# Group A's softmax denominators as pairs of 64-column products, GpSimd's sums of squares tied to the evacuation, and an earlier bias row

## The chip, the cores and the metric

The kernel is one program on 8 cores of one Trainium2 chip. Each core works on its own 2048 of the 16384 positions. The metric is the time of the slowest core, in microseconds on the device; lower is better. A core's own span is about 1 us shorter than the time reported. Some executions fall in a slow state: the cores of one die run at a lower granted clock and the time is 4 to 20% longer. Such executions are left out of all comparisons. In them the cores of the other die are often untouched (granted clock 0.99 or more), and the span of such an *undisturbed core* may still be read. I use the median of these spans, because the slowest of eight cores depends much on chance.

A "unit" below is one step of the attention loop: one head (in group B a pair of heads) by 512 of the core's 2048 queries. Each of the two head groups has 32 units.

## The reference, cut to what matters

```python
# group A: 8 heads of 128, dilated causal attention, mixture of three patterns (window, dilation)
A_PATTERNS = ((128, 1), (512, 4), (2048, 16))
# per pattern: o, running max, l = p.sum(-1) ...
w = l * jnp.exp(mx - mx.max(0))                            # softmax denominators on a common scale
ya = (w[..., None] * o).sum(0) / w.sum(0)[..., None]
# group B: 16 query heads of 64, causal sliding window, two key/value heads, a learned sink per head
# both groups: rms_norm (a sum of squares over all heads of the group), concatenate, project
y = jnp.concatenate([rms_norm(ya, g_mix_a), rms_norm(yb, g_mix_b)], axis=-1)
mix = jnp.einsum('bse,ed->bsd', y, w_out)
x = layer_norm(ALPHA * x + mix); x = layer_norm(ALPHA * x + swiglu(x))
```

What matters: each query needs the sum of its probabilities (the denominator) over all three patterns, the quotient, and the sum of squares of the quotients over all heads.

## The kernel before

A core first makes V and K of both groups, then runs group B's 32 units, group A's 32 units, the out projection, and the feed-forward part. The query projections of later heads (16 products of 512 columns, 3.6 us) are woven into the units to fill TensorE. When they run out, a unit is shorter.

The denominators are made on TensorE, as the probabilities (keys on the rows) times a matrix of ones. In group A the matrix is 128x128, so each denominator appears in all 128 rows, ready to be multiplied elementwise:

```python
        def mm_l():                                        # one pattern of one unit, 1024 columns of p
            ...
            for half in range(2):
                ...
                nc.tensor.matmul(l3[...main part...], k.ones, pm[:, :, :, mo:mo + m], start=st, stop=False)
                ins = nc.tensor.matmul(l3[:, :, me:me + m], k.ones, pe_, start=False, stop=...)   # the short rest
        S_.pe(mm_o, [pb[1], bv_], [k.bBK[b_o]])            # probabilities times V
        S_.pe(mm_l, [pb[1], k.bones], [k.bBK[b_l]])        # probabilities times ones

    def a_evac(h, c):                                      # the unit's end: 1/l = exp(-log l), then the quotient
        S_.act(lambda: nc.scalar.activation(out=ls, in_=lb, func=AF.Ln), [bLB], [bls])
        S_.act(lambda: nc.scalar.activation(out=ls, in_=ls, func=AF.Exp, scale=-1.0), [bls], [bls])
        S_.dve(lambda: nc.vector.tensor_tensor(out=yc, in0=ob, in1=ls, op=ALU.mult), [bOB, bls], [], [byc])
        ...
        sqq.append(lambda: a_square(h, c, yc, byc))        # run in the next unit: ScalarE squares, GpSimd adds

    for u in range(32):                                    # group A
        for p_ in range(3):
            ... next scores ...; a_PV(h, c, pats[p_], ...)
        a_evac(h, c)
        run(dveq, 4)                                       # rope of a projected query, on VectorE
        proj(u + 32 + LEAD, mid=(lambda: reduce_b(u)) if u < 4 else None)
```

`reduce_b` is an fp32 product of ones with group B's sums of squares; it uses the denominators' PSUM bank (`LB`) in the middle of the projections of A's first four units.

The softmax here doesn't subtract the row's maximum and nothing guards it: scores larger than these inputs give would overflow.

## Time and profile before

| | before |
|---|---|
| time, median of 3 runs | 2778.67 us (2778.12 to 2779.98) |
| spans of the cores in the profiled run | 2775.0 to 2779.8 us |
| start to first V product; from there to first K product; from there to first query projection | 13.4; 59.9; 401.2 us |
| query projection and group B | 195.2 us |
| group A: units 0 to 3; 4 to 25; 26 to 31 | 35.7; 166.9; 32.3 us |
| out projection; feed-forward; end | 230.1; 1614.2; 27.6 us |

The rows from the third on are medians over the eight cores of the profiled run, from first product to first product of each stage. The waits of TensorE in group A's first 26 units (view: waits of the slowest core between 660 and 870 us; columns: who waited, for whom, total us, times, longest):

```profile
PE sp L897 <- DVE arena L355: 2.4, 2, 1.2
PE sp L1089 <- DVE arena L1059: 0.5, 1, 0.5
PE sp L1089 <- DVE arena L1051: 0.3, 1, 0.3
```

These are all but a 0.2 us wait in over 200 us, and all of them lie before 677 us: at the end of group B and in A's first unit. The body of A is a closed chain of TensorE work, 7.57 us a unit; only the instructions themselves can shorten it.

### The profile page before, as it was taken

What the parts mean: (1) busy time and instruction counts of PE and PEld (TensorE: products, weight loads), DVE (VectorE), ACT (ScalarE), POOL (GpSimd) and SP (SyncE); (2) the same over time, 40 slices, a digit from 0 to 9 for tenths busy, and PEclk for the clock granted to TensorE, in tenths of its full rate; (3) what the DMA queues carried; (4) which work ended last, traced back from release to release, by engine and by line L of the source; (5) the groups of instructions that cost most, each with busy time, mean ns of one, the idle gap of its engine ahead of it and who ended that gap; (6) DMA issues with size and microseconds to landing.
All of it is one profiled execution on the core that took longest, in us unless ns stands there. A gap on an engine that the chain in (4) does not pass through costs nothing.

```text
span 2779.8 us, 41976 instructions; the slowest of 8 cores (2775.0 to 2779.8 us)
## 1 busy us (share of the span) xinstructions
PE 2722.1 (98%) x14991; PEld 1297.4 (47%) x14991; DVE 1989.9 (72%) x2758; ACT 842.8 (30%) x1229; POOL 569.0 (20%) x588
## 2 busy tenths in 40 slices
PE   8999999999999999999999999999999999999995
PEld 3444444445666444444444444444444444444442
DVE  4756665898888736788866666766988765666767
ACT  0312222787666227333200121111333100112115
POOL 3100000132111557411100011056000000000165
PEclk9999999999999999999999999999999999999998
DMA  9964135568657649799999877888899798555733
GB/s 151 188 117 91 48 86 135 114 121 150 135 133 189 204 138 254 129 157 149 150 165 188 168 112 115 134 210 223 161 172 172 136 200 190 83 88 91 163 125 121
DMA packets 254163, 407.23 MB, mean 146 GB/s; under 512 B 91971, under 2 KB 129988, under 8 KB 253382
## 3 DMA queue, kind: packets, MB, share of 16 engines
q0 software_dynamic: 92336, 193.64, 46.4%
q1 hardware_dynamic: 146070, 179.44, 22.9%
q10 hardware_dynamic: 15552, 31.46, 3.6%
q8 instruction: 122, 2.00, 0.3%
q14 instruction: 83, 0.68, 0.1%
HBM read 490.84 MB, written 104.27 MB: 214 GB/s over the span
## 4 chain that ended last, share of the span: by engine, by line
PE 86%; DMA 6%; DVE 4%; issue 2%; ACT 1%; SPq 0%; DVEq 0%; ACTq 0%; POOLq 0%
PE sp L1565 51%; PE sp L897 8%; PE sp L1371 8%; PE sp L636 6%; PE sp L572 5%; DMA z2s<-arena 3%; PE sp L518 2%; PE sp L1089 1%; DMA vs<-arena 1%; DMA x1h<-arena 1%; PE sp L1107 1%; PE sp L940 1%; PE sp L966 1%; PE sp L616 1%; DMA ka<-arena 1%
## 5 line engine op out<-in xcount | busy, mean ns | idle before, releaser
L1565 PE MATMUL sp<-arena 128*128 128x512 f16 x7408 | 1600.5, 379 | 1.6 <-DVE arena L1839 0.6
L1565 PEld LDWEIGHTS sp<-arena 128*128 128x128 f16 (+1 forms) x7408 | 724.4, 98 | 878.1 <-issue 6.1
L1839 DVE TENSOR_TENSOR arena<-sp,arena 128x512 f32<-128x512 f32 (+1 forms) x348 | 236.6, 689 | 159.9 <-PE sp L1565 143.1
L1925 DVE TENSOR_TENSOR arena<-arena,sp 128x512 f32<-128x512 f32 x257 | 169.7, 683 | 141.6 <-PE sp L1565 141.2
L897 PE MATMUL sp<-arena 128*128 128x512 bf16 x1024 | 236.8, 379 | 3.0 <-DVE arena L355 3.0
L140 POOL DMA_DIRECT2D arena<-wup x88 | 66.5, 756 | 773.0 <-DVE arena L1578 445.6
L1371 PE MATMUL sp<-arena 128*128 128x512 bf16 x1024 | 221.8, 379 | 2.2 <-DVE arena L1360 2.2
L636 PE MATMUL sp<-arena 128*128 128x512 bf16 x1024 | 222.2, 379 | 0.0
L1873 ACT ACTIVATE arena<-sp 128x512 f32<-128x512 f32 x86 | 51.3, 597 | 419.1 <-PE sp L1565 419.1
L362 ACT ACTIVATE arena<-sp,arena 64x512 f32<-64x512 f32 x136 | 92.7, 682 | 274.4 <-PE sp L636 232.4
L1414 POOL TENSOR_TENSOR arena<-arena 128x512 f32<-128x512 f32 x117 | 149.3, 1276 | 113.0 <-DVE arena L1925 74.0
L1413 ACT ACTIVATE arena<-arena 128x512 f32<-128x512 f32 x117 | 73.7, 630 | 283.3 <-DVE arena L1925 136.8
L1586 DVE TENSOR_TENSOR arena<-arena 128x2048 f16<-128x2048 bf16 (+1 forms) x118 | 159.5, 1352 | 0.0
L1371 PEld LDWEIGHTS sp<-arena 128*128 128x128 bf16 x1024 | 100.1, 98 | 124.2 <-issue 4.6
L1578 DVE TENSOR_TENSOR arena<-arena 128x2048 f16<-128x2048 bf16 (+1 forms) x118 | 157.3, 1333 | 0.0
L1839 DVE TENSOR_TENSOR arena<-arena 128x512 f16<-128x512 f32 (+1 forms) x304 | 155.1, 568 | 1.1 <-DMA x1h<-arena 0.9
L636 PEld LDWEIGHTS sp<-arena 128*128 128x128 bf16 x1024 | 99.9, 98 | 119.7
L572 PE MATMUL sp<-arena 128*128 128x512 f16 (+1 forms) x672 | 149.9, 382 | 3.9 <-DVE arena L582 3.7
L1416 POOL TENSOR_TENSOR arena<-arena 128x512 f32<-128x512 f32 x117 | 150.8, 1290 | 9.2 <-ACT arena L1413 8.5
L897 PEld LDWEIGHTS sp<-arena 128*128 128x128 bf16 x1024 | 95.5, 98 | 120.7 <-issue 12.2
L1836 ACT ACTIVATE arena<-sp 128x512 f32<-128x512 f32 x90 | 53.5, 597 | 276.0 <-PE sp L1565 248.5
L1048 ACT ACTIVATE arena<-sp 128x1024 bf16<-128x1024 f32 x96 | 97.4, 1020 | 68.3 <-PE sp L1042 56.5
(153 smaller groups left out, 2601.7 us busy)
## 6 DMA issues: line engine op xcount, KB each, us to landing
arena<-wup POOLq DMA_DIRECT2D x88, 1024.0 KB, 12.7
arena<-wdn POOLq DMA_DIRECT2D x22, 1408.0 KB, 17.3
z2s<-arena SPq DMA_DIRECT2D x39, 512.0 KB, 13.8
arena<-wob SPq DMA_DIRECT2D x32, 512.0 KB, 5.5
arena<-xres SPq DMA_DIRECT2D x32, 512.0 KB, 6.5
x1s<-arena ACTq DMA_DIRECT2D x64, 256.0 KB, 7.0
arena<-z2s SPq DMA_DIRECT2D x29, 512.0 KB, 13.7
arena<-wdb POOLq DMA_DIRECT2D x10, 1408.0 KB, 10.9
```

Source lines behind the costliest of these rows:

```text
L572: ins = nc.tensor.matmul(bank(k, bk), w[:, c, :], m[:, c, :], start=(first and c == 0), stop=(last and c == 7), skip_group_check=True)
L636: ins = nc.tensor.matmul(bank(k, bk), wk[h][:, kc, :], x[:, kc, :], start=(kc == 0), stop=(kc == KC - 1))
L897: ins = nc.tensor.matmul(bank(k, bk), w[:, kc, :], x[:, kc, :], start=(kc == 0), stop=(kc == KC - 1))
L1048: S_.act(lambda: nc.scalar.activation(out=p, in_=sp[:, :], func=AF.Exp, scale=scA), spb[s], [bp])
L1371: ins = nc.tensor.matmul(bank(k, bk), w[:, kc, :], y[:, kc, hh * 512:(hh + 1) * 512], start=(first and i == 0), stop=(last and i == len(kc ...
L1414: S_.pool(lambda: nc.gpsimd.tensor_tensor(out=za, in0=za, in1=z, op=ALU.add), [bz, bza], [bza])
L1416: ss["pend"] = [lambda: S_.pool(lambda: nc.gpsimd.tensor_tensor(out=qa, in0=qa, in1=sq, op=ALU.add), [bsq, bqa], [bqa])]
L1565: ins = nc.tensor.matmul(bank(k, bk), w, x, start=(first and i == 0), stop=(last and i == len(ws) - 1), skip_group_check=True)
L1578: S_.dve(lambda: nc.vector.tensor_tensor(out=v, in0=w[:, 0:n, :], in1=w[:, n:2 * n, :], op=ALU.add), [bw], [b])
L1586: S_.dve(lambda: nc.vector.tensor_tensor(out=v, in0=w[:, :, 0:128], in1=w[:, :, 128:256], op=ALU.subtract), [bw], [b])
L1839: S_.dve(lambda: nc.vector.tensor_tensor(out=o, in0=a, in1=b, op=op), [ba, bb], [bo])
L1925: S_.dve(lambda: nc.vector.tensor_tensor(out=v, in0=v, in1=o, op=op), [b, bo], [b])
```

## The change

The intent, in four parts.

1. In 26 of A's 32 units the ones matrix becomes 64 columns wide, and the unit's queries are split in two halves whose products run side by side in the two column halves of the array. Half as many columns are streamed.
2. The denominators then lie as 64 rows x 256 columns per half. The evacuation becomes a log of 128x256 written back to PSUM and four exponentials of 64x256.
3. GpSimd's additions of squares in both groups wait for the end of the exponential of the next evacuation, so that they no longer collide with VectorE's masks.
4. At the start, the V bias row is loaded first, in one transfer, and V's outgoing tiles get a ring of nine buffers in place of five.

```diff
@@ start
+    S_.dma("sp", k.bvrow[0][0:1, :], k.bv_d, [], [k.bvrow[1]], "bv")          # now ahead of five small loads
...
-                ct["v"] = nx("vo", 5)
+                ct["v"] = nx("vo", 9)
@@ group B's and group A's sums of squares (A's shown)
-                S_.pool(lambda: nc.gpsimd.tensor_tensor(out=ac, in0=ac, in1=sq, op=ALU.add), [SQ[1], bacc[c]], [bacc[c]])
+                poolq.append(lambda bls: S_.pool(lambda: nc.gpsimd.tensor_tensor(... same ...), [SQ[1], bacc[c], bls], [bacc[c]]))
@@ group A's denominators
+    L2 = 26
...
+            def mm(e, o_, r, stop):
+                ins = nc.tensor.matmul(o_, k.ones[:, 0:64], r, start=st[e], stop=stop, skip_group_check=True)
...
+            for half in range(2):
...
+                for e in range(2):
+                    mm(e, le[e][:, :, mo:mo + 128 - m]..., pm[:, :, ae[e], mo:mo + m], False)
+                for e in range(2):
+                    ins = mm(e, le[e][:, :, me:me + m], pe_[:, ae[e]], last and half == 1)
...
-        S_.pe(mm_l, [pb[1], k.bones], [k.bBK[b_l]])
+        S_.pe(mm_l2 if 4 * h + c < L2 else mm_l, [pb[1], k.bones], [k.bBK[b_l]])
@@ evacuation
+        if 4 * h + c < L2:
+            S_.act(lambda: nc.scalar.activation(out=lb[:, 0:256], in_=lb[:, 0:256], func=AF.Ln), [bLB], [bLB])
+            for i, (e, d) in enumerate(((0, 0), (0, 1), (1, 0), (1, 1))):
+                S_.act(lambda e=e, d=d: nc.scalar.activation(out=ls[64 * d:64 * d + 64, 256 * e:256 * e + 256],
+                             in_=lb[64 * e:64 * e + 64, 0:256], func=AF.Exp, scale=-1.0), [bLB], ...)
+        else:
...                                                                           # as before
+        while poolq:
+            poolq.pop(0)(bls)
```

More of the change, by code (lines that the diff above doesn't have):

```diff
@@ L327, in persist @@
     assert P.o <= FREE
+    o = XO + 2 * X_SLOT
+    k.bvrow = (view(k, o, VW, F32), S_.buf("bvrow", o, o + 4 * VW))
+    S_.dma("sp", k.bvrow[0][0:1, :], k.bv_d, [], [k.bvrow[1]], "bv")
+    S_.dve(lambda: nc.vector.memset(k.onesf, 1.0), [], [k.bonesf])
     for v, d in ((k.bqk, k.bqk_d), (k.bsw, k.bsw_d), (k.gmix, k.gmix_d), (k.lnp, k.lnp_d), (k.esink, k.sinks_d)):
@@ L330, in persist @@
     S_.dve(lambda: nc.vector.memset(k.ones, 1.0), [], [k.bones])
-    S_.dve(lambda: nc.vector.memset(k.onesf, 1.0), [], [k.bonesf])
-    S_.act(lambda: nc.scalar.activation(out=k.esink, in_=k.esink, func=AF.Exp), [bs], [bs])
-    S_.dve(lambda: nc.vector.tensor_scalar(out=k.gmix, in0=k.gmix, scalar1=32.0, scalar2=None, op0=ALU.mult), [bs], [bs])
 XO = 4096
@@ L422, in phase1 @@
     xq, bxq = P("xq", 8 * 256, F16)
+    o_r = P.o
     xr, bxr = P("xr", 16 * 256, F16)
@@ L471, in phase1 @@
         S_.dma("pool", wk[h], k.wk_d[h], [], [bwk[h]], "wk%d" % h)
-    S_.dma("sp", T1[0][0][0:1, :], k.bv_d[:, 0:512], [], [T1[0][1]], "bv0")
-    S_.dma("sp", T1[1][0][0:1, :], k.bv_d[:, 512:1024], [], [T1[1][1]], "bv1")
-    S_.dma("sp", T2[0][0][0:1, 0:128], k.bv_d[:, 1024:1152], [], [T2[0][1]], "bv2")
-    for i, (v, b, n) in enumerate((T1[0] + (512,), T1[1] + (512,), T2[0] + (128,))):
-        S_.pe(lambda i=i, v=v, n=n: nc.tensor.matmul(bank(k, 7 - i)[:, 0:n], k.onesf[0:1, :], v[0:1, 0:n], start=True, stop=True),
-              [b, k.bonesf], [k.bBK[7 - i]])
+    for i, n in enumerate((512, 512, 128)):
+        S_.pe(lambda i=i, n=n: nc.tensor.matmul(bank(k, 7 - i)[:, 0:n], k.onesf[0:1, :], k.bvrow[0][0:1, 512 * i:512 * i + n], start=True, stop=True),
+              [k.bvrow[1], k.bonesf], [k.bBK[7 - i]])
         S_.act(lambda i=i, n=n: nc.scalar.activation(out=bv[:, 512 * i:512 * i + n], in_=bank(k, 7 - i)[:, 0:n], func=AF.Copy),
                [k.bBK[7 - i]], [bbv] if i == 0 else [], [bbv] if i else [])
+    bs = k.bsmall
+    S_.act(lambda: nc.scalar.activation(out=k.esink, in_=k.esink, func=AF.Exp), [bs], [bs])
+    S_.dve(lambda: nc.vector.tensor_scalar(out=k.gmix, in0=k.gmix, scalar1=32.0, scalar2=None, op0=ALU.mult), [bs], [bs])
     k.bvs, k.bka, k.bkb = [], [[] for _ in range(8)], []
@@ L488, in phase1 @@
           for t, o in ((0, XO + 2 * X_SLOT), (1, o_g))]
+    VW9 = VO + [(view(k, o_r + 2048 * i, 1024), S_.buf("vx%d" % i, o_r + 2048 * i, o_r + 2048 * i + 2048)) for i in range(4)]
     def v_part(t, q, bk):
@@ L495, in v_part @@
             if g == 0:
-                ct["v"] = nx("vo", 5)
-            vo, bvo = VO[ct["v"]]
+                ct["v"] = nx("vo", 9)
+            vo, bvo = VW9[ct["v"]]
             S_.dve(lambda: nc.vector.tensor_tensor(out=vo[:, c], in0=bank(k, bk), in1=p[:, c], op=ALU.add), [k.bBK[bk], bp],
@@ L696, in phase1 @@
     S_.dma("pool", k.perm, k.perm_d, [], [k.bperm], "perm")
+    bxr = S_.buf("xr", o_r, o_r + 8192)
     G[:] = [(v, S_.buf("g%d" % i, o_g + 8192 * i, o_g + 8192 * i + 8192)) for i, (v, _) in enumerate(G)]
@@ L871, in phase2 @@
     sqq = []
+    poolq = []
     peq = []
@@ L995, in sq_acc @@
             S_.act(lambda: nc.scalar.activation(out=sq, in_=src, func=AF.Square), [bsrc], [SQ[1]])
-            S_.pool(lambda: nc.gpsimd.tensor_tensor(out=av, in0=av, in1=sq, op=ALU.add), [SQ[1]] + bacc, bacc)
+            poolq.append(lambda bls: S_.pool(lambda: nc.gpsimd.tensor_tensor(out=av, in0=av, in1=sq, op=ALU.add), [SQ[1], bls] + bacc, bacc))
     k.bys = [None] * KC
@@ L1091, in mm_o, with mm_l2 @@
             return ins
+        def mm_l2():
+            st = [first, first]
+            def mm(e, o_, r, stop):
+                ins = nc.tensor.matmul(o_, k.ones[:, 0:64], r, start=st[e], stop=stop, skip_group_check=True)
+                st[e] = False
+                return ins
+            le = [lb[64 * e:64 * e + 64, 0:256].rearrange("p (a m) -> p a m", a=2) for e in range(2)]
+            ae = [slice(2 * e, 2 * e + 2) for e in range(2)]
+            if pat == 2:
+                p4 = p.rearrange("p (a f n) -> p a f n", a=4, f=2)
+                for f in range(2):
+                    for e in range(2):
+                        ins = mm(e, le[e], p4[:, ae[e], f, :], last and f == 1)
+                return ins
+            n, w, m = (3, 128, 32) if pat == 1 else (15, 32, 8)
+            pm = p[:, 2 * w:1024].rearrange("p (j a m) -> p j a m", j=n, a=4)
+            for half in range(2):
+                pe_ = p[:, w * (1 - half):w * (1 - half) + w].rearrange("p (a m) -> p a m", a=4)
+                mo = m * half
+                me = 128 - m if half == 0 else 0
+                for e in range(2):
+                    mm(e, le[e][:, :, mo:mo + 128 - m].rearrange("p a (j m) -> p j a m", j=n), pm[:, :, ae[e], mo:mo + m], False)
+                for e in range(2):
+                    ins = mm(e, le[e][:, :, me:me + m], pe_[:, ae[e]], last and half == 1)
+            return ins
         def mm_l():
@@ L1118, in a_evac @@
         ob, lb, bOB, bLB = bank(k, b_o), bank(k, b_l), k.bBK[b_o], k.bBK[b_l]
-        S_.act(lambda: nc.scalar.activation(out=ls, in_=lb, func=AF.Ln), [bLB], [bls])
-        S_.act(lambda: nc.scalar.activation(out=ls, in_=ls, func=AF.Exp, scale=-1.0), [bls], [bls])
+        if 4 * h + c < L2:
+            S_.act(lambda: nc.scalar.activation(out=lb[:, 0:256], in_=lb[:, 0:256], func=AF.Ln), [bLB], [bLB])
+            for i, (e, d) in enumerate(((0, 0), (0, 1), (1, 0), (1, 1))):
+                S_.act(lambda e=e, d=d: nc.scalar.activation(out=ls[64 * d:64 * d + 64, 256 * e:256 * e + 256], in_=lb[64 * e:64 * e + 64, 0:256],
+                                                             func=AF.Exp, scale=-1.0), [bLB], [] if i else [bls], [bls] if i else [])
+        else:
+            S_.act(lambda: nc.scalar.activation(out=ls, in_=lb, func=AF.Ln), [bLB], [bls])
+            S_.act(lambda: nc.scalar.activation(out=ls, in_=ls, func=AF.Exp, scale=-1.0), [bls], [bls])
+        while poolq:
+            poolq.pop(0)(bls)
         if h < 7:
@@ L1145, in a_square @@
             else:
-                S_.pool(lambda: nc.gpsimd.tensor_tensor(out=ac, in0=ac, in1=sq, op=ALU.add), [SQ[1], bacc[c]], [bacc[c]])
+                poolq.append(lambda bls: S_.pool(lambda: nc.gpsimd.tensor_tensor(out=ac, in0=ac, in1=sq, op=ALU.add), [SQ[1], bacc[c], bls], [bacc[c]]))
     def reduce_a(t):
```

## The prediction

> **What bounds the kernel now.** I read the page's busy line first, then the stretches (busy time by window), then the waits of TensorE by stage, then the timeline of one unit per stage, because the change touches four stages: the start, group B's attention, group A's attention, and the few units that end it.
>
> The busy line, and two stretches of A (columns: stretch, length, then PE, PEld, DVE, ACT, POOL busy):
>
> ```profile
> PE 2722.1 (98%) x14991; PEld 1297.4 (47%) x14991; DVE 1989.9 (72%) x2758; ACT 842.8 (30%) x1229; POOL 569.0 (20%) x588
> ...
> 740.00:800.00 60.00, 60.00 (x682) 40.08 (x679) 50.95 (x71) 36.20 (x48) 11.16 (x10) 1.00 0.65 147
> ...
> 870.00:917.00 47.00, 39.23 (x463) 26.12 (x462) 41.34 (x60) 31.52 (x45) 9.54 (x7) 1.00 0.89 249
> ```
>
> TensorE is the bound, with 58 us idle in the span. In the body of A it never idles: a unit takes 7.57 us and only fewer or shorter TensorE instructions shorten it. In A's last 47 us, where no projections are left, it idles 7.8 us behind VectorE (88% busy). There VectorE's work counts.
>
> One unit of A, the last pattern's denominators (L1107, L1110), then the evacuation:
>
> ```profile
> 740.32 0.37 PE L1107 MATMUL sp<-arena 128*128 128x480 bf16 x1
> 740.52 0.18 PE L1110 MATMUL sp<-arena 128*128 128x32 bf16 x1
> 740.55 0.36 PE L1107 MATMUL sp<-arena 128*128 128x480 bf16 x1
> 740.75 0.18 PE L1110 MATMUL sp<-arena 128*128 128x32 bf16 x1
> 740.78 3.61 PE L897 MATMUL sp<-arena 128*128 128x512 bf16 x16
> 741.04 1.23 DVE L1051 TENSOR_TENSOR arena<-arena 128x1024 bf16<-128x1024 bf16 x1
> 741.29 0.60 ACT L1119 ACTIVATE arena<-sp 128x512 f32<-128x512 f32 x1
> 741.98 0.63 ACT L1120 ACTIVATE arena<-arena 128x512 f32<-128x512 f32 x1
> ```
>
> Start to start, this pattern's ones products hold TensorE 740.78 - 740.32 = 0.46 us; the same reading gives 0.43 (two 512-column products, L1098) and 0.44 us for the other two patterns: 1.33 us a unit.
>
> Group B already makes its ones products as 64-column pairs, so it prices the new form:
>
> ```profile
> 594.21 0.61 PE L940 MATMUL sp<-arena 64*128 64x128 bf16 x10
> 594.75 0.63 PE L966 MATMUL sp<-arena 128*64 128x128 bf16 x10
> 595.21 0.60 PE L982 MATMUL sp<-arena 128*64 128x384 bf16 x8
> 595.75 1.90 PE L897 MATMUL sp<-arena 128*128 128x512 bf16 x8
> ```
>
> Each of the first three blocks streams 1024 columns in each half of the array. A 512-column product takes 0.2155 us, so 1024 take 0.43. The blocks take 0.54, 0.46 and 0.54 us. The middle one, followed by the same shape of array (128*64), costs 0.03 over; the two after which the shape changes cost 0.11 over. In the individual starts every pair lies 3 ns apart, so the halves do run side by side, and each of the three changes of shape in a unit (128*128 to 64*128, to 128*64, to 128*128) costs 0.093 to 0.098 us.
>
> **What the Trainium skill says.** "TensorEngine Tiling (Array Packing)", Key Properties: a change of tiling mode drains TensorE. The trace agrees, at about 0.095 us. Same page, Restrictions: column tiling turns fast weight load off; the trace has 110 ns for a 64-column load against 98 for a 128-column one. "SBUF — State Buffer", Who interferes with whom: a VectorE instruction with two SBUF inputs and a GpSimd one that reads SBUF block each other whole. The trace agrees: A's first mask (L1051) takes 0.69 us alone and up to 1.76 when GpSimd's sum of squares (L1146, 1.27 us) runs. "TensorE: Matmul & The Clock Gate", Part 1: a cold array runs at half rate for about 3.4 us of work. Here 512 columns take 0.427 us for 8 us, from 9.05 to 17.3.
>
> **The change part by part.**
>
> (a) A's denominators, 26 of 32 units. Columns halve: 1.33 us a unit would become 0.65, and 26 x 0.68 = 18 us would be gained if nothing else happened. But each pattern's block stands between full-array products, so each now has two changes of shape: 6 x 0.095 = 0.57 us a unit. The short pairs (64 and 16 columns) also cannot go below a pair's weight load; I take 0.055 us from B's 128-column pairs. So: first pattern 0.095 + 2 x 0.108 + 0.095 = 0.40; second 0.19 + 0.082 + 0.055 + 0.082 + 0.027 = 0.44; third 0.19 + 0.102 + 0.055 + 0.102 + 0.007 = 0.46. Sum 1.30 against 1.33: 0.03 us a unit, 0.8 us in all. The gain is eaten by the switches.
>
> (b) The evacuation in these units: a log of 256 columns in place of 512, then four exponentials of 64x256 in place of one of 128x512. ScalarE takes 598 ns for 512 columns from PSUM and 1020 for 1024, so 0.82 ns a column and 387 ns for 256; two in a row overlap by 0.1 us. Log 0.39, gap 0.09, exponentials 3 x 0.29 + 0.39 = 1.26: ready 1.74 us after the log starts, against 0.69 + 0.63 = 1.32. VectorE's product comes 0.4 us later; it idled 0.8 us in the same unit waiting for ScalarE, so that is hidden. The bank of the denominators, though, comes free after 1.74 us in place of 0.60. The next unit needs it 3.9 us later: hidden. In A's first four units it is needed sooner, for the reduction of B's sums of squares in the middle of the projection (L1158):
>
> ```profile
> 702.05 1.89 PE L897 MATMUL sp<-arena 128*128 128x512 bf16 x8
> 702.40 0.60 ACT L1119 ACTIVATE arena<-sp 128x512 f32<-128x512 f32 x1
> 703.09 0.63 ACT L1120 ACTIVATE arena<-arena 128x512 f32<-128x512 f32 x1
> 703.78 1.02 PE L1158 MATMUL sp<-arena 128*128 128x512 f32 x2
> ```
>
> The bank would be free at 702.40 + 1.74 = 704.14 against 703.78: with a semaphore's delay about 0.4 us of stall. The first of the four units also waits for GpSimd's last sum of B, which now starts after the evacuation. Four times 0.4: a loss of 1.7 us.
>
> (c) GpSimd's sums start with the end of the exponential, when VectorE runs the product from PSUM and the rope (one SBUF input each). In B and the body of A this frees VectorE, but TensorE is the bound: nothing. In the last six units it counts:
>
> ```profile
> 877.46 1.27 POOL L1146 TENSOR_TENSOR arena<-arena 128x512 f32<-128x512 f32 x1 [6.74 <-ACT arena L1142]
> 877.52 1.75 DVE L1051 TENSOR_TENSOR arena<-arena 128x1024 bf16<-128x1024 bf16 x1
> ...
> 879.43 0.61 PE L1089 MATMUL sp<-arena 128*128 128x128 bf16 x8 [0.74 <-DVE arena L1051]
> ```
>
> Five such collisions (877.5, 888.7, 894.4, 898.8, 903.2) of about 1.05 us each are followed by TensorE waits of 0.74 + 1.20, 0.76, 0.59, 0.75 + 0.23 and 1.05 of 1.36: 5.3 us at most. ScalarE becomes the next bound, and VectorE, behind in these units, will still hit some of the moved sums with another two-input operation. I take half: 2.5 us gained.
>
> (d) The start.
>
> ```profile
> 3.40 1.23 SPq L140 DMA_DIRECT2D arena<-bv  x3
> ...
> 9.05 4.17 PE L476 MATMUL sp<-arena 1*128 1x512 f32 x6 [9.05 <-DMA arena<-bv]
> ```
>
> The V bias row was issued behind five small loads and landed at 9.0; now it is the first DMA, and the first one here lands 1.7 us after its issue. So its broadcast can run from about 3 to 7 us, under the loads. By the landings in the trace the first x and weight chunks are there at 8.6, and the first four at 17.1. The second x tile's first part lands at 20.3, where TensorE wants it at 22.07. So the 4 us in front shrink to at most 1.8: the loads take over as the limit. Later landings have 2 to 5 us of slack, so the gain stays. I take 1.5. The longer ring of V stores removes 10.7 us of VectorE waits that no TensorE wait follows: nothing.
>
> Sum: -0.8 + 1.7 - 2.5 - 1.5 = -3.1 us; 2778.7 becomes 2775.5.
>
> **The rivals.**
> (1) Switches hide: if the drain overlapped in A, (a) would give up to 18 us and the time be near 2760. For it: the halving is real and limiting the form to 26 units looks tuned. Against: B pays each change 32 times over.
> (2) The evacuation becomes a wait: if four 64-row exponentials take more than my 1.26 us (the 64-row ones in the rope, L362, take 682 ns for 512 columns, no less than 128 rows), VectorE's product and then the masks come late in every unit; 0.3 us x 26 would give some 2786. VectorE's freed 0.55 us a unit (mask L1051) speaks against.
> (3) The start and the tail give nothing, because DMA or ScalarE take their place: 2779 to 2780, the loss of (b) alone.
> (4) The short pairs cost more or less than 0.055 us: 0.03 us on six pairs or so is another 3 to 5 us either way.
>
> **Range and chances.** A fifth of rival 1 (some switches partly hidden) would be 2772; rivals 3 and 4 together 2782. I take 2769 to 2781. 2% is 55.6 us, three times all that (a) could ever give: faster 0.01, slower 0.01, same 0.98.
>
> **What would show it.** (a) ones blocks of 0.40 to 0.46 us start to start, in pairs 3 ns apart, with about 0.1 us on each side; a unit in the body of A still 7.5 to 7.6 us. (b) TensorE waits of some 0.4 us before the fp32 reduction in A's first units, named after ScalarE or GpSimd. (c) L1051 at 0.69 us everywhere, TensorE idle in the last 47 us down from 7.8 to some 5. (d) V's first product at about 8.7 in place of 13.15, but a wait on x or its weights until some 20.3. The prediction is wrong if a unit in the body of A is below 7.3 or above 7.8 us.

## The result, and the profile after

| | before | after |
|---|---|---|
| time, median of 3 runs | 2778.67 us | **2785.30 us** (2783.95 to 2786.02) |
| undisturbed cores, median span | 2775.5 (256 cores) | 2781.1 (24 cores) |
| start to V; V to K; K to projection | 13.4; 59.9; 401.2 | 9.3; 62.6; 397.0 |
| group B with its projections | 195.2 | 195.2 (one core 200.0) |
| A: units 0 to 3; 4 to 25; 26 to 31 | 35.7; 166.9; 32.3 | 39.9; 170.8; 30.0 |
| out projection; feed-forward; end | 230.1; 1614.2; 27.6 | 231.5; 1614.1; 29.6 |

The ratio is 1.0022, with a 95% interval of 0.9999 to 1.0045. A ratio here is always the mean time of one kernel's fast runs over that of the other's in the same rounds, so it is not quite the ratio of the medians quoted. By the 2% limit this is "same", but the time lies 6.6 us above the one before and outside the predicted range. The last figure of the last row says little: the end stage varies by 2 to 4 us from core to core within a run.

The busy line of the page after, and the two stretches of A on one core (columns as in the prediction):

```profile
PE 2727.7 (98%) x15251; PEld 1296.3 (47%) x15251; DVE 1966.1 (71%) x2758; ACT 859.9 (31%) x1307; POOL 569.3 (20%) x588
...
740.00:800.00 60.00, 59.48 (x733) 38.39 (x732) 46.58 (x69) 40.42 (x70) 11.14 (x10) 1.00 0.65 144
870.00:917.00 47.00, 39.52 (x503) 26.83 (x502) 37.92 (x60) 33.90 (x49) 9.38 (x7) 1.00 0.87 251
```

VectorE lost 24 us of busy time, as intended (A's first mask takes 0.69 us everywhere; no more collisions with GpSimd), but TensorE is 5.6 us busier, and in the body of A it now idles 0.5 us in 60, where before it never did. The waits of TensorE in the same part of A (same view as before, same columns):

```profile
PE sp L1203 <- ACT arena L1159: 1.7, 3, 0.6
PE sp L1039 <- DVE arena L359: 1.4, 5, 0.3
...
PE sp L1203 <- POOL arena L1002: 1.0, 1, 1.0
```

Three new waits: the fp32 reduction (L1203) waits three times for the exponentials and once for GpSimd, and five times the next head's scores (L1039) wait for rope (L359). The evacuation of one unit:

```profile
740.64 0.39 ACT L1157 ACTIVATE sp<-sp 128x256 f32<-128x256 f32 x1
741.12 1.55 ACT L1159 ACTIVATE arena<-sp 64x256 f32<-64x256 f32 x4
...
742.84 0.69 DVE L1171 TENSOR_TENSOR arena<-sp,arena 128x512 bf16<-128x512 f32 x1 [1.04 <-ACT arena L1159]
```

The exponentials take 1.55 us for four, with no overlap, and VectorE's product starts 742.84 - 740.33 = 2.51 us after the projection (which starts at 740.33). Before, the projection of this unit started at 740.78 (shown in the prediction), and the product 2.02 us after it and without a wait:

```profile
742.80 0.68 DVE L1126 TENSOR_TENSOR arena<-sp,arena 128x512 bf16<-128x512 f32 x1
```

The ones blocks of the changed kernel, on the same core:

```profile
744.28 0.61 PE L1099 MATMUL sp<-arena 128*128 128x128 bf16 x8
744.83 0.41 PE L1107 MATMUL sp<-arena 128*64 128x256 bf16 x4
745.17 0.72 PE L1039 MATMUL sp<-arena 128*128 128x128 bf16 x8
...
747.65 0.44 PE L1107 MATMUL sp<-arena 128*64 128x240 bf16 x8
748.02 0.39 PE L903 MATMUL sp<-arena 128*128 128x512 bf16 x1
```

The block as such is short: 745.17 - 744.83 = 0.34 us, and 748.02 - 747.65 = 0.37, where the blocks before held TensorE 0.43 to 0.46. But a block has a drain on each side, and in the individual starts two more costs: the first pair after a switch is 0.023 us longer than the second (0.130 against 0.107 for 256 columns), and the first weight load after the switch back is up to 0.05 us longer than others. With everything up to the next regular start, the three blocks cost 0.486, 0.472 and 0.474 us, against 0.431, 0.437 and 0.460 before: 0.10 us a unit more. The unit itself went from 7.575 to 7.685.

Finally, every fourth unit of the body takes 8.03 us, and units 1 to 3 take 9.36 each in place of 8.43. The fp32 reduction in the first two units:

```profile
674.28 1.10 PE L1203 MATMUL sp<-arena 128*128 128x512 f32 x2 [1.00 <-POOL arena L1002]
...
683.63 1.10 PE L1203 MATMUL sp<-arena 128*128 128x512 f32 x2 [0.58 <-ACT arena L1159]
```

At the start, the bias row's broadcast and the first V product:

```profile
2.66 4.18 PE L475 MATMUL sp<-arena 1*128 1x512 f32 x6 [2.66 <-DMA arena<-bv]
...
9.24 3.31 PE L522 MATMUL sp<-arena 128*128 128x512 bf16 x8 [2.40 <-DMA arena<-wv]
```

The row is there at 2.66 us in place of 9.05, and the first V product now waits for its weights, as predicted.

### The profile page after: what moved, and what is told of

Read it like the earlier page. It is cut to its first block, busy times and chain, and to the rows that moved or that the text cites. A ratio compares the mean times of both kernels' runs of the same rounds, so it can differ in the third digit from the quotient of the medians.

```text
span 2784.3 us, 42572 instructions; the slowest of 8 cores (2778.6 to 2784.3 us)
## 1 busy us (share of the span) xinstructions
PE 2727.7 (98%) x15251; PEld 1296.3 (47%) x15251; DVE 1966.1 (71%) x2758; ACT 859.9 (31%) x1307; POOL 569.3 (20%) x588
## 3 DMA queue, kind: packets, MB, share of 16 engines
q8 instruction: 124, 2.03, 0.3%
## 4 chain that ended last, share of the span: by engine, by line
PE 91%; DVE 2%; ACT 2%; issue 2%; SPq 1%; DMA 1%; POOL 0%; DVEq 0%; ACTq 0%; POOLq 0%
PE sp L1610 57%; PE sp L640 8%; PE sp L1416 8%; PE sp L903 6%; PE sp L576 5%; PE sp L522 1%; SPq L140 1%; PE sp L1099 1%; PE sp L1107 1%; DMA ys<-arena 1%; ACT arena L1056 1%; PE sp L1039 1%; DMA arena<-xT 1%; PE sp L620 1%; PE sp L661 1%
```

## The experiments

**Theory.** Three things made the time longer: the switches of array shape cost more than the halved columns save; the longer evacuation turned slack into waits (every fourth unit, and the reductions in the first units); and the tie gains nothing, since what it gives in A's last units is taken back later. The start alone is a gain. **Rivals.** The waits come from the products' new timing and not from the evacuation; or the tie, not the pairs, makes the loss; or the time is scattered over the cores by chance.

Four of the runs below (e_evac, e_sblog, e_group2, e_group3) were made on a chip that was throttled in other stages (the kernel before took 3002 us beside them). In them stage A ran at a granted clock of 0.98 to 1.00 and is read; their totals are not. The first four kernels of what follows ran on one chip, beside a kernel before of 2778.67 us (median of 7).

### One part at a time

**e_noones**: the changed kernel with the old denominators and evacuation, so the start and the tie alone.

```diff
-    L2 = 26
+    L2 = 0
```

> The changed kernel with the new form of the denominators switched off (limit of units 26 set to 0; start, V ring and GpSimd tie stay). Theory A, the new form costs 8 us in group A and the rest gains: some 2771 to 2773, a unit in the body of A back at 7.57 us, A's last units still 30 us. Rival B, the form is neutral (as predicted) and the tie of GpSimd's sums is what slows A: stays at 2783 to 2786, body unit 7.68.

**e_ones**: the kernel before with parts 1 and 2 alone (pairs and evacuation as in the diff).

> The kernel before with the new form of the denominators and its evacuation alone. Theory A: some 2786 to 2788 (before + 8), body unit 7.68 with every fourth some 8.0. Rival B: 2778 give or take 2, body unit 7.57.

**e_pool**: the kernel before with part 3 alone (both `S_.pool` lines become `poolq.append`).

> The kernel before with GpSimd's sums tied to the evacuation alone. Theory A: A's last six units 2 us shorter, the first four up to 1 us longer, 2777 to 2778. Rival B: 2783 or more.

**e_start**: the kernel before with part 4 alone.

> The kernel before with the early bias row and the longer V ring alone. Both theories: group B's first projection starts 5 to 6 us earlier, total 2773 to 2774. If the gain were taken back later (a transfer), 2777 or more.

Measured:

| | time of the fast runs, us | ratio (95%) | undisturbed cores, median | A: 0-3; 4-25; 26-31; out |
|---|---|---|---|---|
| e_noones | 2781.9, 2783.4, 2784.2 | 1.0017 (1.0001 to 1.0034) | 2774.0 (32) | 36.6 to 37.8; 166.8; 29.9; 231.7 to 233.4 |
| e_ones | 2785.5 to 2787.4 | 1.0029 (1.0012 to 1.0046) | 2782.7 (28) | 40.2; 170.8; 32.3; 229.9 |
| e_pool | 2780.9, 2782.8 | none | 2776.8 (24) | 36.6; 166.8; 29.9; 232.4 |
| e_start | 2774.9 to 2776.5 | 0.9990 (0.9974 to 1.0007) | 2772.8 (28) | 35.7; 166.9; 32.3; 230.1 |

One reading of the table needs care. In e_ones the first four units take 40.2 to 40.8 us on five cores and 38.5 on three. On those five the granted clock is 0.83 between 669 and 679 us, on the other three 1.00: for some 3 us of the first projection each 512-column product takes 0.43 us in place of 0.22. That costs 1.7 us in the first unit, comes and goes from core to core in other runs too, and is not a price of the pairs as such; their part in these units is 38.5 - 35.7 = 2.8 us.

In e_noones the body of A is back at 7.57 us for every unit, in e_ones it is at 7.685 and 8.02 as in the changed kernel. So the whole loss in A's body belongs to parts 1 and 2. On the median core the pairs cost 2782.7 - 2775.5 = +7.2, the tie +1.3 and the start -2.7; the sum, +5.8, agrees with the +5.6 of the whole change. The tail's gain of 2.4 us is there with the tie (29.9 against 32.3), and the out projection gives 2.3 back.

A surprise: the times of e_noones do not fit its cores. Its median core is faster than the kernel before, its slowest core is not: 5 of 32 cores come 5 to 9 us after their median. I return to this below.

### Switches and waits apart

**e_evac**: the changed kernel with the new evacuation, but the old ones products. The result is wrong (relative error 0.028): only the timing counts.

```diff
-        S_.pe(mm_l2 if 4 * h + c < L2 else mm_l, [pb[1], k.bones], [k.bBK[b_l]])
+        S_.pe(mm_l, [pb[1], k.bones], [k.bBK[b_l]])
```

> Wrong output on purpose. The changed kernel with the old full-array ones products, but with the new evacuation as it is (log of 256 columns, four exponentials of 64x256): the new waits without the switches of array shape. Theory A (two separate costs): a unit in the body of A back at 7.57 us, yet every fourth still some 0.3 us longer (rope behind the late product), and A's units 1 to 3 still 0.6 to 0.8 us over 8.43. Rival (the switches alone cause all): every fourth unit 7.57 and units 1 to 3 at 8.43.

Measured (stage A): body 7.57, every fourth unit 8.02, units 1 to 3 9.29. The 0.11 us a unit belongs to the pairs, the long fourth unit and nearly all of the loss in the first units to the evacuation. The wait is the same one as in the changed kernel (TensorE's waits, 700 to 860 us):

```profile
PE sp L1039 <- DVE arena L359: 1.0, 4, 0.3
```

The first rival falls.

**e_sblog**: the log goes to a buffer in SBUF in place of the PSUM bank, so the bank is free 1.5 us earlier.

```diff
-            S_.act(lambda: nc.scalar.activation(out=lb[:, 0:256], in_=lb[:, 0:256], func=AF.Ln), [bLB], [bLB])
+            lo, blo = LS[ct["ls"] % 2]
+            S_.act(lambda: nc.scalar.activation(out=lo[:, 0:256], in_=lb[:, 0:256], func=AF.Ln), [bLB], [blo])
```

> The changed kernel with the log written to SBUF, so that the denominators' bank is free after the log. Theory A: A's units 1 to 3 lose their wait for the exponentials (9.36 to some 8.7 us); the body stays 7.68, every fourth 8.0, as the exponentials end no sooner. Rival (the bank holds up the body too): the body falls to 7.57.

Measured: units 1 to 3 at 8.54, which is the old 8.43 plus the 0.11 of the pairs. So the held bank is the whole of the other 0.82 us there. But every fourth unit became longer (8.29): VectorE waits 1.26 us a unit for the exponentials there, against 0.98 in e_evac. Why they come later was not followed up.

**e_group2**: the ones of a unit's first two patterns in one block, so four switches a unit in place of six.

```diff
+        if 4 * h + c < L2:
+            onesq.append(lambda: S_.pe(mm_l2, [pb[1], k.bones], [k.bBK[b_l]]))
+            if pat in (1, 0):
+                run(onesq, 3)
```

> The changed kernel with the ones products of the first two patterns issued as one block: four changes of array shape a unit in place of six. If each pair of changes costs what the changed kernel's trace shows (about 0.095 + 0.023 on entry, 0.098 and a slower first weight load on exit, 0.23 us together), a body unit is 7.45 us. If the extra 0.11 us came from the form itself (short pairs, slow weight loads), it stays 7.65 or more.

Measured: body 7.42 us, as expected (7.45), read from one projection to the next:

```profile
738.65 3.63 PE L904 MATMUL sp<-arena 128*128 128x512 bf16 x16
...
744.08 0.63 PE L1108 MATMUL sp<-arena 128*64 128x256 bf16 x12
744.65 0.63 PE L1046 MATMUL sp<-arena 128*128 128x128 bf16 x5
...
746.07 3.63 PE L904 MATMUL sp<-arena 128*128 128x512 bf16 x16
```

Two switches, there and back, are thus worth 7.685 - 7.42 = 0.265 us, not the 0.19 of the prediction. If each costs the same, three such round trips are 0.80 us a unit, so the halved columns save 7.575 + 0.80 - 7.685 = 0.69, which is the 0.68 of the prediction. Every fourth unit stayed at 8.14: it is held by a chain of waits and not by TensorE's work.

**e_group3**: all three patterns' ones in one block, with a fifth buffer for probabilities; two switches.

```diff
-        return PT[nx("p", 4)]
+        return PT[nx("p", 5)]
...
+            if pat in (0,):
+                run(onesq, 3)
```

> All three patterns' ones products in one block a unit, a fifth probability buffer: two changes of shape. By the same reckoning a body unit of 7.22 us; if the form itself costs, 7.6 or more. Every fourth unit still longer by its wait.

A miss: body 7.83 us, longer than with six switches. The block itself is fine, but look at what precedes it (timeline of one unit):

```profile
739.12 0.65 PE L1101 MATMUL sp<-arena 128*128 128x32 bf16 x17 [0.46 <-DVE arena L1069]
...
739.70 0.88 PE L1109 MATMUL sp<-arena 128*64 128x256 bf16 x20
740.51 1.69 PE L905 MATMUL sp<-arena 128*128 128x512 bf16 x7
```

All 20 products of the unit take 740.51 - 739.70 = 0.81 us from start to start, where the three blocks of the changed kernel take 0.34 + 0.35 + 0.37 = 1.06. But TensorE waits 0.46 us for the last mask. The ones blocks between the patterns had been the work that covered the latency of exponential and mask.

### Mending it

**e_mend**: e_group2, with rope put ahead of the late product in every fourth unit, the fp32 reduction after the projection, and A's first K and V loaded earlier. **e_mendold**: the same last two with the old denominators.

```diff
+        if c == 3:
+            run(dveq, 4)
...
-        proj(u + 32 + LEAD, mid=(lambda: reduce_b(u)) if u < 4 else None)
+        proj(u + 32 + LEAD)
+        if u < 4:
+            reduce_b(u)
```

> The changed kernel mended where the runs so far point: the first two patterns' ones products in one block, the rope's last two steps ahead of the product in every fourth unit, the reduction of B's sums after the projection, and A's first keys and values loaded at B's unit 16 in place of 20. Expected: body 7.42 in all units (A's units 4 to 25 some 163.5 us against 166.9), units 1 to 3 some 8.2, no 4 to 6 us stall of single cores in B; total 2768 to 2771. If the stall in B is not the y store queued behind the V loads, one core in eight still shows B at 199 or more.

> The same without the new form of the denominators (old full-array products and evacuation): body 7.57, units 1 to 3 8.43; total 2771 to 2773, 3 us over the mended form. If the form gains nothing even when mended, it is the faster of the two.

Measured, beside a kernel before of 2780.0 us (medians of the fast runs): e_mend 2778.9 (ratio 0.9998, 0.9979 to 1.0018), e_mendold 2779.2 (0.9997, 0.9977 to 1.0016). Two of the mends missed. Every fourth unit stayed at 8.15: the scores that wait are issued in the unit c = 3, and so need a rope that ran in c = 2; I had put it one unit too late. Moving the reduction to the end made units 1 to 3 8.97 in place of 9.0 and unit 4 longer as well.

**e_rope2**: the changed kernel with rope first in the right unit.

```diff
+        if c == 2:
+            run(dveq, 4)
         a_evac(h, c)
```

> The changed kernel with one move: in the third unit of each head, rope's last steps go ahead of the denominator's product on VectorE. If every fourth unit is longer because the next head's scores wait for rope, and rope stands behind the late product: every fourth unit falls from 8.03 to about 7.69 like the others, units 4 to 25 from 170.8 to about 169.1; units 1 to 3 stay at 9.36. Rival, that the wait only moves to the next scores' own evacuation: 8.0 stays.

Measured (one execution, 2786.77 us): the fourth unit of a head fell from 8.03 to between 7.68 and 7.71, and the third, which now runs rope first, rose from 7.68 to between 7.74 and 7.88. So the wait was the one that the trace named. And yet units 4 to 25 took 170.85 us, exactly as before the mend: one single unit, the eleventh of the stage, went from 7.76 to 9.10 on every core. There the tie put GpSimd's addition into rope's way:

```profile
756.17 1.26 POOL L1191 TENSOR_TENSOR arena<-arena 128x512 f32<-128x512 f32 x1 [6.42 <-ACT arena L1159]
756.28 2.03 DVE L359 TENSOR_TENSOR arena<-arena 128x512 bf16<-128x512 f32 x1
```

Rope's last addition, two SBUF inputs, takes 1.03 to 1.08 us everywhere else in the stage. Here GpSimd started 0.11 us ahead of it, and it took 2.03. In five other units of this core rope started 0.15 to 0.42 us ahead, and GpSimd was the one that became longer: 1.77 to 2.04 us in place of 1.27. The tie is a rule about when GpSimd may start, tuned to the old order of VectorE's work; with another order it brings about the collision it was made to avoid.

**e_final**: the kernel before with the new start, the pairs grouped as in e_group2, rope first in c = 2, the log to SBUF in the first head only, and no tie. **e_start2**: the start alone again, on the same chip in the same rounds.

> The kernel before with the bias row and the V ring, and the paired ones products with what the runs so far say is wrong with them mended: ones of the first two patterns in one block (four switches in place of six), rope's last steps ahead of the denominator's product in the unit before the one that waits (the earlier try sat one unit too late), logarithm to SBUF in the first head only, so that the bank is free for the fp32 reduction, and no tie of GpSimd. If the switches and the waits are the whole cause: body units 7.42, every fourth unit 7.42 to 7.6 (8.14 with the waits), units 1 to 3 about 8.3 (9.0), units 4 to 25 about 163.5 (166.8 before, 170.8 after), units 0 to 3 about 35.5, and a total of 2770 to 2773, some 4 us under the start alone on the same chip. Rival, that the out projection takes back what stage A gains, as it did with the tail: the body is quicker, the total within 1 us of the start alone. Rival, that another wait takes the place of rope in the fourth unit: it stays at 8.0 or more and units 4 to 25 at 166 to 167.

> The kernel before with the bias row and the ring of nine V tiles only, a repeat of the earlier run with more rounds, as the yardstick of the next run. Expected: median 2774 to 2777, ratio 0.999, stage A as before (units 1 to 3 at 8.43, body 7.57, units 4 to 25 in 166.8).

Measured: e_final 2776.3 and 2777.5 us in its two fast runs; e_start2 2776.1 median of four, ratio 0.9989 (0.9976 to 1.0002). On the median core both have 2772.4 us. In e_final the body is at 7.42, units 1 to 3 at 8.28, and every fourth unit at 7.9, where it now waits for the product itself (0.28 us), since rope stands ahead of it. Units 4 to 25 take 165.8 us against 166.8. Even with its waits mended, the paired form is worth 1 us in its main stage, and that does not reach the total: units 0 to 3 together are 0.5 to 1.2 us longer on five of the eight cores (and 0.5 shorter on the other three). On three of these five it is the first unit at a lower granted clock again (0.83 between 669 and 679 us, 1.00 on the rest); the second unit of the other two is 0.9 and 1.5 us longer, for reasons not followed up. The first rival of its expectation (no gain in the total) holds, though not for the reason given: the out projection was the same, 230.1. The second (another wait takes the place of rope) comes close too, with 7.9 and 165.8 us.

### The start, halved

**e_ring** and **e_bias**: the kernel before with the V ring alone, and with the bias row alone (one look each).

> The kernel before with the longer V ring alone. If the ring removes the 2.4 us wait of TensorE near 139 us (VectorE behind, as the V stores held it up): from the first K product to the first projection 397 to 398 us in place of 399 to 403; first V product still at 13. If the ring does nothing, as predicted: as in the kernel before.

> The kernel before with the early bias row alone: first V product at 8.5 to 10 us in place of 13, V stage 2.5 to 3 us longer as it waits for x and weights, so 1.3 to 1.8 us gained at the first K product; from there on as in the kernel before (399 to 403 us) if the rest of the start's gain is the ring's.

Measured (totals 2780.5 and 2779.8 us, each with one or two late cores, so not read). First K product at 71.5 us with the bias row against 73.4 before: 1.8 us gained, and the ring alone leaves it at 72.8. From there to the first projection: 398.7 us with the bias row alone, 398.2 to 398.5 in e_ones and e_pool, which have neither, and 396.9 to 397.5 in the eleven kernels with the ring that ran undisturbed there. So the ring is worth 1 to 1.5 us. (The profile of before had 401.2 there, more than any later run.) Where it comes from is to be seen in TensorE's waits between 60 and 480 us in the kernel before:

```profile
PE sp L572 <- DVE arena L582: 3.7, 3, 2.4
```

This is the slowest core; the eight cores have 1.6 to 4.3 us of it. In e_ring five cores have none and three 0.5 to 1.6.

### The late cores

Counted over all runs, the cores that came more than 4 us after the median of their own kernel are 17 of 192 where group B has the tie, and 9 of 480 where it has not. With the tie in B, 10 of 21 fast executions had a late core, and the slowest core is the time. (The loss of the changed kernel does not come from there: of the tied kernels, those with the pairs had 1 late core in 60, those without 16 in 132.) The next three runs shared one chip, beside a kernel before of 2779.7 us (median of its seven fast runs).

**e_tieb**: the new start, old denominators, and the tie in group B alone. **e_tiea**: the same with the tie in group A alone.

```diff
 e_tieb: a_square
-                poolq.append(lambda bls: S_.pool(...))
+                S_.pool(lambda: nc.gpsimd.tensor_tensor(...), [SQ[1], bacc[c]], [bacc[c]])
 e_tiea: sq_acc
-            poolq.append(lambda bls: S_.pool(...))
+            S_.pool(lambda: nc.gpsimd.tensor_tensor(...), [SQ[1]] + bacc, bacc)
```

> The kernel before with the new start, and GpSimd's sums tied to the evacuation in group B's units alone. So far, over undisturbed cores of all runs: the start alone has a median core of 2772.6 us and none of 68 cores over 4 us above its median; the start with the whole tie has 2774.0 and 5 of 32 cores more than 4 us above (2779 to 2783), which sets the time of the slowest core. If the stalls come from the tie in B (they show as B stages of 200 to 202 us in place of 195.2, and in the first unit of A as a wait for GpSimd): units 0 to 3 of A 36.55, tail 32.15, some cores 4 to 9 us late, total 2779 to 2784. Rival, that the late cores are a matter of chance (a DMA) and not of the tie: no core over 2777, total 2776 to 2778.

> The same start with the tie in group A's units alone. If the tie's harm sits in B: no late cores beyond those of the start, units 0 to 3 of A near 35.7, tail 29.85, out projection 231.4 to 233.4 (the tail's gain given back), total 2775 to 2777, as the start alone. If the late cores come from the tie wherever it is: 2779 or more here too.

| | time, us | ratio (95%) | undisturbed cores: median; over 4 us late | A: 0-3; 26-31; out |
|---|---|---|---|---|
| e_tieb | 2777.3 to 2785.3 | 1.0002 (0.9989 to 1.0016) | 2774.5; 5 of 44 | 37.4; 32.2; 230.1 |
| e_tiea | 2774.8 to 2775.8 | 0.9983 (0.9969 to 0.9997) | 2772.3; 0 of 52 | 35.7; 29.9; 232.4 |

The harm sits in group B. There the tie makes A's first unit 0.8 to 2 us longer, since GpSimd's last addition for B has to wait for A's first evacuation, and the late cores are there. In group A alone the tie is harmless, and useless: the tail gains 2.3 us and the out projection loses 2.3. Why it loses them is to be seen on one core of each kernel, first without the tie (e_start2), then with it in A (e_tiea):

```profile
899.72 0.69 DVE L1134 TENSOR_TENSOR arena<-sp,arena 128x512 bf16<-128x512 f32 x1 [0.43 <-ACT arena L1125]
901.29 0.69 DVE L1149 TENSOR_TENSOR arena<-arena 128x512 f32<-128x512 f32 x1 [0.88 <-ACT arena L1147]
901.90 15.98 DVE L1365 SCALAR_TENSOR_TENSOR arena<-arena 128x512 bf16<-128x512 bf16 x24
...
907.43 1.89 PE L1376 MATMUL sp<-arena 128*128 128x512 bf16 x8 [0.83 <-DVE arena L1365]
```

```profile
896.65 0.69 DVE L1174 TENSOR_TENSOR arena<-sp,arena 128x512 bf16<-128x512 f32 x1 [1.43 <-ACT arena L1163]
898.78 0.69 DVE L1189 TENSOR_TENSOR arena<-arena 128x512 f32<-128x512 f32 x1 [1.44 <-ACT arena L1187]
899.39 15.98 DVE L1405 SCALAR_TENSOR_TENSOR arena<-arena 128x512 bf16<-128x512 bf16 x24
...
904.92 1.89 PE L1416 MATMUL sp<-arena 128*128 128x512 bf16 x8 [2.39 <-DVE arena L1405]
```

The out projection needs the normalised group outputs, and VectorE makes those one after the other, 24 in a run in both kernels. Counted from the tail's first product (867.4 and 865.6 us, from each core's own timeline), TensorE begins the out projection 2.3 us sooner with the tie (29.8 us in place of 32.2), but VectorE begins its run only 0.7 us sooner (33.8 in place of 34.5): before its last two steps of the tail it now waits 1.43 and 1.44 us for ScalarE, in place of 0.43 and 0.88. In both kernels the fourth block of the projection can go on 5.5 us after the run's start, so with the tie it waits 2.39 us in place of 0.83. That is 1.6 us of the loss. The rest falls on four of the eight cores of e_tiea: their granted clock is 0.83 between 905 and 915 us, that of the others 1.00, and they take 233.1 to 233.4 us for the stage, the others 231.4 to 231.7.

How a late core comes about is shown in part. Six profiled cores with a stage B of 200 to 203 us, in kernels with the tie and without, have the same stall near its end (this one is core 7 of e_pool):

```profile
650.87 1.00 DVE L1012 TENSOR_TENSOR arena<-sp,arena 128x512 bf16<-128x512 f32 x1 [4.69 <-DMA ys<-arena]
```

VectorE's product waits 3.6 to 6.6 us for an earlier output tile to land in memory. That store comes late because it is issued late. This is SyncE's queue on the same core, and then on core 5 of the same run, which has no stall (vs: loads of A's first V; ys: the stores):

```profile
621.23 11.05 SPq L140 DMA_DIRECT2D arena<-vs  x2
632.38 9.29 SPq L140 DMA_DIRECT2D ys<-arena  x2
```

```profile
621.08 4.60 SPq L140 DMA_DIRECT2D arena<-vs  x1
625.77 16.54 SPq L140 DMA_DIRECT2D ys<-arena  x2
```

The program puts the loads of A's first K and V, at B's unit 20, ahead of the store in this queue, and on core 7 the store's turn comes 6.6 us later. The 108 undisturbed profiled cores with the load at that place agree: SyncE was done issuing this store 167.2 to 170.2 us after the first query projection on the six late cores, and at most 164.7 us after it on the 95 whose stage B takes 195.2 us (the seven between take 195.5 to 197.1). With the load at unit 16, e_mend had no late core in 28 and e_mendold 2 in 32; the one of these that was profiled waits 5.2 us for its store at 629.4 us, some 20 us before the six: the stall moved with the load. Why the loads take longer to issue on some cores, and how the tie makes that more frequent, stays open.

**e_notie**: the changed kernel without the tie.

> The changed kernel without the tie: the new start and the paired ones. If the three parts add up on the median core (start -2.8, paired ones +7.3, tie +1.4, from the runs so far; the whole change +5.7): median core 2775.4 - 2.8 + 7.3 = 2779.9, no core over 4 us above that, total 2782 to 2784. If the parts depend on each other (the tie's GpSimd wait in A's first unit is there only with the pairs, or the pairs hide the start's gain): off by more than 1 us.

Measured: 2783.37 us (ratio 1.0012, 0.9997 to 1.0027), median core 2779.7 against 2779.9 expected. The three parts add up. (One core of 32 came 4.2 us after the median, where none was expected; it has the stall described above.)

**What is best.** e_tiea has the lowest median (2775.4), and its ratio of 0.9983 lies wholly below 1; but its median core (2772.3) is that of the start alone (2772.6 over 68 cores), so the tie in A can go as well. The part of this change worth keeping is its start: about 2.8 us a core, 0.1%. It shows on the median core; the ratio of the slowest cores (0.9989, 0.9976 to 1.0002) alone would not exclude that nothing is gained.

## Why the prediction was wrong, point by point

The sum of the prediction was -3.1 us; the median core shows +5.6, the slowest +6.6. By its own steps:

**(a), the pairs in the body: the mechanism was right, a term was mis-sized.** The drains are there and eat the gain. But 0.19 us for a switch there and back was read from group B's blocks as "0.03 over" and "0.11 over", and only the drains were carried into the sum. Group B's individual starts already showed the first pair after a switch to 128*64 at 0.080 us against 0.053 to 0.056 for the next (starts 594.750, 594.830 and 594.886), which I overlooked. With that and the slow first weight load, a round trip costs 0.265 us (e_group2 against the changed kernel), three times a unit. The short pairs erred the other way: 0.055 us was taken because of the weight load, and a 64-column pair took 0.029 us (starts 746.358 and 746.387 on the core shown). In all, -0.03 became +0.11 us a unit.

**(b), "hidden": the step that failed.** The exponentials were taken as 1.26 us, with an overlap of 0.1 us; they took 1.55 without any. "VectorE's product comes 0.4 us later; it idled 0.8 us, so that is hidden" looked at the product alone. These 0.8 us are idle time before the next mask (L1057), behind the product and rope, and that mask was indeed not held up. But behind the product in VectorE's queue stands rope, and in every fourth unit the next head's scores need rope: 7.68 became 8.03 (e_evac shows it without the pairs, e_rope2 takes it away). Together, (a) and this cost 3.9 us in units 4 to 25, where the prediction had a gain of 0.8. The stall in units 1 to 3 was predicted at 0.4 us; 0.58 was named by the trace and the whole held bank is worth 0.82 (e_sblog). Units 1 to 3 lost 2.8 us, and the first unit, with its wait for GpSimd (1.0 us), which was foreseen but not sized, 1.4: together 4.2 us and not 1.7. With (d) at -2.8 and the rest of (c), the tail and the out projection, set to zero, that is 3.9 + 4.2 - 2.8 = +5.3 of the +5.6 measured.

**(c), the tie: right where it looked, wrong on the whole.** The masks are at 0.69 us and the tail gained 2.3 of the 2.5 predicted. But the chain that follows was not asked: the gain was counted up to the end of the tail, and VectorE's normalisation behind it sets when the out projection can go on. That run began only 0.7 us sooner, since VectorE now waits for ScalarE, which the prediction did name as the next bound. "In B ... nothing" failed too: A's first unit pays there, and the late cores come with it.

**(d), the start: the bias row as predicted (1.5 against 1.8), the ring not.** "No TensorE wait follows" was a misreading: in the kernel before TensorE waits 1.6 to 4.3 us a core for VectorE between 60 and 480 us, in e_ring 0 to 1.6, and the ring gave 1 to 1.5 us.

**The rivals.** (Two sums of the prediction are 0.1 us off by rounding: four times 0.4 is 1.6, and 2778.7 - 3.1 is 2775.6. Nothing hangs on them.) Rival 2 named the right mechanism, the longer evacuation, and even the size (2786), but with every unit waiting and on ScalarE's time per row; in truth one unit in four waits, for what is queued behind. It was set aside because VectorE had slack on average. Rival 1 was rightly refused. The range of 2769 to 2781 was too narrow, because its upper end added no wait of VectorE's queue.

## What to carry to other kernels

A gain in streamed columns on TensorE has to be set against the full price of each change of array shape, measured as the time up to the next regular start and not as the drain alone; grouping the blocks pays only as long as they are not what covers another engine's latency. When an operation comes later on an engine with slack, follow what is queued behind it to the rarest consumer: the slack of the average unit says nothing about the one unit in four that waits. And a gain at the end of a stage counts only after asking which engine sets the start of the next.

## What the Trainium skill lacked or had wrong

- "TensorEngine Tiling (Array Packing)", Key Properties, says that a change of mode drains TensorE but gives no price. Here a change to 128*64 and back costs 0.265 us in all (body 7.685 against 7.42 us with one round trip fewer): two drains of about 0.095, and the rest on the first pair (0.130 against 0.107 us for 256 columns) and on the first weight load after the return.
- "ScalarE: Activation LUTs", What ACT_TABLE_LOAD costs, states that back-to-back activations overlap by about 93 ns. Other neighbours in this trace do (one of 1016 ns from 739.74 us, the next from 740.64: 0.11 us), but the four 64x256 exponentials from PSUM do not: each takes 376 to 381 ns, and they start 387 to 393 ns apart. Its 186 ns plus 0.833 ns a column would be 399 ns for 256 columns, which is 18 to 23 ns more than they took with 64 rows and 13 more than the log took with 128 (386 ns).
- No page that I read warns that a store can land late on one core of eight because loads ahead of it in SyncE's queue take longer to issue there (here the store's turn came at 632.4 us against 625.8); 10 of the 21 fast executions with the tie in group B had a late core.
